# Four planning passes for the order of operations of a hybrid decoder step

## The chip, the cores and the metric

The kernel runs on one core of a Trainium2 chip. A core has five engines with an instruction list of their own: TensorE (PE; its weight loads PEld), VectorE (DVE), ScalarE (ACT), GpSimd (POOL) and SyncE (SP), which here issues the DMAs. Each works its list in order and waits for the others by semaphores. The metric is device time in microseconds of one execution, the median of several. Lower is better.

## The reference

Two groups of tokens (32 sample tokens and 512 of the prompt in each, T = 544 columns, the prompt's halves one after the other) pass two layers with D = 2048, all in fp32:

```python
def mixer_layer(x, ...):
    h = rmsnorm(x, norm_g)
    z = h @ w_in                       # 2048 x 5120
    u_a, v_a, g_a, q, k, v, g_b, u_c, g_c = jnp.split(z, splits, axis=-1)
    q, k = rope(q), rope(k)
    out_a = chunk_mlp(u_a, v_a, w_s, b_s)
    out_b = swa(q, k, v, sinks)        # window of 128, 16 heads, 4 kv heads
    out_c = s5(u_c, h0, ...)           # complex scan over the tokens, gelu, glu
    mixed = concat[out_a * silu(g_a), out_b * silu(g_b), out_c * silu(g_c)]
    return x + mixed @ w_out
```

A last RMSNorm gives y. New keys, values, chunk rows and scan states are outputs too.

## The kernel before

**Tiling.** Activations lie transposed: 16 tiles of 128 features by 544 tokens. An fp32 product is made of three fp32r products: each operand is split into a rounded part `hi` and a rest `lo` (ScalarE writes `hi`, VectorE subtracts), and hi·hi, hi·lo and lo·hi are added in PSUM. Weights are split when they arrive (tiles `wr` raw, `wh` and `ks` split); activations are split once per group (`gen_rows`, tiles `s`). For each layer and each of the two groups of tokens the code records:

- `input_tiles`: single output tiles, 16 contraction steps each (`project`), with the branches (attention, S5, chunk) recorded between them from generators in lanes. In the very first stage three tiles share the PSUM banks and are multiplied by the row `rstd` afterwards (`mul(t[:, sl], ps[h], rstd[:, sl])` and the rope of the keys); `rstd` itself is made from the same loaded rows (`gen_first`). `gen_tables(l)` builds the S5 tables of a layer with many small VectorE operations; layer 0's are recorded during the first stage, layer 1's during the second group's input stage of layer 0.
- `input_pairs` and then `output_tiles`: pairs of output tiles by seven half products (`product_pair`), 21 matmuls of 272 columns for each of 8 contraction steps, in seven PSUM banks. The first group of a layer also builds the weight sums on VectorE (`add(r[...])`, tile `wr`) and stores them; the second loads them back (`si`, `so`). At the end of a pair ScalarE copies the first product out (tile `e`), and VectorE's adds free the other banks one after the other. The next group's row splits are recorded from `after(k)`, which is called within a pair's steps, so ahead of that pair's adds.

**The order.** No instruction is issued while this is recorded. Line 202, `take`, stores each operation with its predecessors (by overlapping reads and writes, and by who had a buffer before) and a rank, `k - self.lead`, its place in the record less a lead. Weight loads and splits have a lead of 150 places, of 300 at the start of a stage (`rec.ahead(AHEAD)`, lines 860 and 907). Line 233, `times`, gives each a duration: `end`, until its result is there, and `step`, until its engine takes the next. Line 280, `order`, is a list scheduler: it steps through modelled time, and an engine that is free takes the lowest rank among the operations that are ready by then. An operation on another engine becomes ready `WAKE` after the end of what it waits for (32 to 65 ns). It has a model of the port that VectorE and GpSimd share, of a slower TensorE after a pause, of the DMA queue, and of ScalarE's table loads. Line 353, `give`, issues everything in that order; line 357 is the call, so all instructions of the profile carry L357 and are told apart by tile names. What is given to an engine stays in that order on the chip.

Of the kernel before, what the change touches and what calls it, by code (L numbers as in the profile page):

```python
# [75 lines left out]
ROW = {t: r for r, t in enumerate(ROWS)}  # L76
OUT_SINGLE = 2

SUMS_AT = 6
RES = 8  # L80
OUTRES = 4
# [54 lines left out]
class Recorder:  # L136
# [2 lines left out]

    ENGINES = ("SP", "Activation", "PE", "DVE", "Pool")  # L140

    WAKE = {"DVE": 32, "Activation": 32, "Pool": 65, "PE": 50, "SP": 50}
    TABLES = {AF.Exp: 0, AF.Tanh: 0, AF.Sin: 1, AF.Sqrt: 2, AF.Sigmoid: 3, AF.Silu: 4}

    class Engine:
# [133 lines left out]

    def order(self):  # L280

        n = len(self.ops)
        after = [[] for _ in range(n)]
        for k, preds in enumerate(self.preds):
            for j, written in preds.items():
                after[j].append((k, written))
        left, at = [len(p) for p in self.preds], [0.0] * n
        ready, come, free = ({e: [] for e in self.ENGINES}, {e: [] for e in self.ENGINES}, {e: 0.0 for e in self.ENGINES})
        for k in range(n):
            if not left[k]:  # L290
                heapq.heappush(ready[self.ops[k][0]], (self.ops[k][4], k))
        port = queue = idle = 0.0
        cold, table, events, out, flying = -1.0, None, [0.0], [], []
        while events:
            now = heapq.heappop(events)
            while events and events[0] <= now:
                heapq.heappop(events)
            for e in self.ENGINES:
                while come[e] and come[e][0][0] <= now + 1e-6:
                    k = heapq.heappop(come[e])[1]  # L300
                    heapq.heappush(ready[e], (self.ops[k][4], k))
            for e in self.ENGINES:
                if free[e] > now + 1e-6 or not ready[e]:
                    continue

                if e == "SP" and len(flying) >= 8 and flying[-8] > now:
                    heapq.heappush(events, flying[-8])
                    continue
                k = ready[e][0][1]
                end, step, lock, more = self.ops[k][5]  # L310
                if lock and e in ("DVE", "Pool") and port > now + 1e-6:
                    heapq.heappush(events, port)
                    others = [x for x in ready[e] if not self.ops[x[1]][5][2]]
                    if not others:
                        continue
                    ready[e].remove(min(others))
                    heapq.heapify(ready[e])
                    k = min(others)[1]
                    end, step, lock, more = self.ops[k][5]
                else:  # L320
                    heapq.heappop(ready[e])
                if lock:
                    port = now + step
                if e == "PE":

                    if now - idle > 1500 and now > 20000:
                        cold = now + (3400 if now - idle < 3500 else 6800)
                    if now < cold:
                        end, step = end * 1.6, step * 1.7
                    idle = now + step  # L330
                elif e == "SP":
                    queue = max(now + 600, queue) + more
                    end = queue + 1400 - now
                    flying.append(now + end)
                elif e == "Activation" and more is not None:
                    if more != table:
                        end, step = end + 1283, step + 1283
                    table = more
                out.append(k)
                free[e] = now + step  # L340
                heapq.heappush(events, free[e])
                for s, written in after[k]:
                    es = self.ops[s][0]
                    t = now + (step if es == e and (e == "PE" or e != "SP" and not written) else end + self.WAKE[es])
                    at[s] = max(at[s], t)
                    left[s] -= 1
                    if not left[s]:
                        heapq.heappush(come[es], (at[s], s))
                        heapq.heappush(events, at[s])
        assert len(out) == n  # L350
        return out

    def give(self, tc):
        with tc.manual_schedule():
# [6 lines left out]
def hybrid_step(ctx: ExitStack, tc: tile.TileContext, a, o):  # L361
# [14 lines left out]
    class Slots:  # L376
# [22 lines left out]
        def put(self, *xs):  # L399
            for x in xs:  # L400
                self.free.append(self.held.pop(id(x))[1])
# [387 lines left out]
    def gen_rows(source, scales, order, xs, acc, keep, norm):  # L789


        if norm is not None:
            rs = tt()
            SP.dma_start(rs, rs_d[norm])
        for n, k in enumerate(order):
            t = source(k)
            scale = None if scales is None else scales[:, k:k + 1]
            if norm is not None:
                V.scalar_tensor_tensor(out=t, in0=t, scalar=scale, in1=rs, op0=ALU.mult, op1=ALU.mult)
                SP.dma_start(xn_d[k], t)  # L800
                scale = None
                if n == KT - 1:
                    put(rs)
            if k < 8:
                xs[k] = [half(), half()]
                for h, sl in HS:
                    split(xs[k][h], t[:, sl], scale)
            else:
                xs[k] = row(t, scale)
            if acc is not None:  # L810
                sum_squares(t, acc, n == 0, t)
            if keep is None:
                put(t)
            else:
                keep[k] = t
            yield
# [83 lines left out]
    def project(tiles, xs, order=range(KT), ready=None, ps=None, first=0):  # L900

        ps = ps or [[mm_t.get() for h in range(2)] for _ in tiles]
        order = list(order)[:4 * len(tiles[0])]
        for c in range(len(tiles[0])):
            for n, chunks in enumerate(tiles):
                r, w = raw.part(), hl.part()
                with rec.ahead(FIRST_AHEAD if c < first else AHEAD):
                    SP.dma_start(r, chunks[c].rearrange("p (k m) -> p k m", k=4))
                    S.activation(w[:, 0], r, AF.Copy)
                    V.tensor_tensor(out=w[:, 1], in0=r, in1=f32(w[:, 0]), op=ALU.subtract)  # L910
                for j in range(4):
                    if ready is not None:
                        ready(order[4 * c + j])
                    x = xs[order[4 * c + j]]
                    for i, (p, q) in enumerate(((0, 0), (0, 1), (1, 0))):
                        for h in range(2):
                            TE.matmul(ps[n][h], w[:, p, j, :], x[h][q], start=c + j + i == 0, stop=4 * c + j == len(order) - 1 and i == 2)
                tick()
        return ps
# [418 lines left out]
    def input_tiles(l, g, X):  # L1338
# [9 lines left out]
        while n < len(order):  # L1348
# [81 lines left out]
            if two[-1] == (GLU_AFTER if l + g else ("va", 1)):  # L1430
# [17 lines left out]
                put(*ub)  # L1448
            if len(order) - n == SUMS_AT:
                lanes["ops"].add(X.sums(RES))  # L1450
# [276 lines left out]
```

## Time and profile before

| | |
|---|---|
| median of 3 runs | 3124.15 us (3121.15 to 3125.85) |
| profiled execution | 3125.5 us, span 3123.8 us |
| TensorE busy | 2962.7 us, 95%, 24208 matmuls |
| VectorE busy | 2400.8 us, 77% |
| ScalarE busy | 1567.3 us, 50% |
| GpSimd busy | 103.1 us, 3% |
| mean granted TensorE clock | 0.98 |
| HBM traffic | 610 MB, 195 GB/s over the span |

Busy time is the time in which an engine has at least one instruction at work. The clock is the share of TensorE's full clock that was granted: 1.00 is 2.4 GHz, 0.50 is 1.2 GHz, and a mean over a stretch lies between. The span runs from the first to the last instruction. Tile names are cut of their numbers: `s` are the general buffers, `e` those near the PSUM banks, `mm`, `sc` and `bk` PSUM banks, `wr`, `wh` and `ks` weights, `x`, `xn`, `br`, `mix` DRAM tensors.

### The profile page before, as it was taken

To read this page: it belongs to the slowest core of one execution; us is meant where nothing else is said; L and a number is where in the kernel's file an instruction comes from. 1 tells how busy PE (TensorE), PEld (TensorE's weight loads), DVE (VectorE), ACT (ScalarE), POOL (GpSimd) and SP (SyncE) were. 2 spreads that over 40 slices of the span, in tenths; PEclk is the share of its full clock that TensorE was granted. 3 is DMA by queue.
4 is the path that set the end of the run, shared out by engine and by line. 5 is a ranking of instruction groups with operands and counts; after the bars stand their busy time and mean duration, and the time that the engine had idled before them with its cause. 6 is when DMAs were issued, how large, how long until landed. Compare 5 with 4: busy or idle time off the path is not lost. (4 is left out here: it accounts for less than half of the span.)

```text
span 3123.8 us, 64427 instructions
## 1 busy us (share of the span) xinstructions
PE 2962.7 (95%) x24208; PEld 2880.1 (92%) x24208; DVE 2400.8 (77%) x4856; ACT 1567.3 (50%) x3106; POOL 103.1 (3%) x280
## 2 busy tenths in 40 slices
PE   5999999999898999999999999999999999999996
PEld 5988999989888899999999899999998999999996
DVE  9778789898997876668675877779887687556866
ACT  4347644453444764445443665335444475544643
POOL 0010000000010000000001000000000000000000
PEclk8999999999999999999999999999999999999998
DMA  5554376757964527667695335666679554667665
GB/s 176 182 165 124 100 247 232 241 188 238 309 196 131 153 85 231 197 227 227 219 315 148 108 111 173 223 227 227 212 255 315 162 150 137 199 199 232 214 216 174
DMA packets 394842, 614.29 MB, mean 197 GB/s; under 512 B 82209, under 2 KB 139169, under 8 KB 394529
## 3 DMA queue, kind: packets, MB, share of 16 engines
q1 hardware_dynamic: 394528, 610.17, 61.6%
q8 instruction: 189, 3.10, 0.4%
q14 instruction: 125, 1.02, 0.1%
HBM read 439.64 MB, written 170.38 MB: 195 GB/s over the span
## 5 line engine op out<-in xcount | busy, mean ns | idle before, releaser
L357 PE MATMUL mm<-s,wh 128*128 128x272 f32 x12660 | 1849.7, 293 | 67.6 <-ACT wh L357 23.2
L357 PEld LDWEIGHTS mm<-s,wh 128*128 128x128 f32 x12660 | 1695.8, 191 | 90.3 <-ACT wh L357 29.8
L357 ACT ACTIVATE wh<-wr 128x896 fp32r<-128x896 f32 (+1 forms) x719 | 567.5, 795 | 762.0 <-PE mm L357 511.2
L357 DVE TENSOR_TENSOR wh<-wr,wh 128x896 fp32r<-128x896 f32 (+1 forms) x719 | 640.2, 895 | 321.8 <-ACT wh L357 306.5
L357 PE MATMUL sc<-s,wh 128*128 128x272 f32 x2346 | 513.0, 290 | 0.8 <-DVE e L357 0.7
L357 DVE TENSOR_TENSOR s<-s,s 128x544 f32<-128x544 f32 (+11 forms) x738 | 387.7, 552 | 35.5 <-DMA yd<-s 9.9
L357 PE MATMUL mm<-s,ks 128*128 128x272 f32 x2316 | 388.2, 289 | 6.1 <-ACT ks L357 3.0
L357 PEld LDWEIGHTS sc<-s,wh 128*128 128x128 f32 x2346 | 384.3, 190 | 2.9 <-DVE e L357 2.7
L357 PEld LDWEIGHTS mm<-s,ks 128*128 128x128 f32 x2316 | 327.3, 189 | 9.1 <-DVE e L357 3.7
L357 ACT ACTIVATE ks<-wr 128x896 fp32r<-128x896 f32 x193 | 183.2, 949 | 235.4 <-PE mm L357 131.7
L357 DVE TENSOR_TENSOR ks<-wr,ks 128x896 fp32r<-128x896 f32 x193 | 209.9, 1088 | 108.5 <-ACT ks L357 97.5
L357 PE MATMUL sc<-s,ks 128*128 128x272 f32 x1158 | 258.5, 290 | 1.1 <-DVE e L357 0.9
L357 PE MATMUL bk<-s,wh 128*128 128x272 f32 x1125 | 256.7, 291 | 2.7 <-DVE e L357 2.6
L357 DVE TENSOR_TENSOR wr<-wr 128x256 f32<-128x256 f32 (+1 forms) x432 | 219.2, 508 | 39.6 <-DMA wr<-w_inp 21.2
L357 ACT ACTIVATE s<-s 128x544 fp32r<-128x544 f32 (+4 forms) x320 | 171.2, 555 | 102.1 <-DVE s L357 60.8
L357 ACT ACTIVATE s<-s,mx 128x128 f32<-128x128 f32 x512 | 177.5, 389 | 34.2 <-DVE mx L357 33.8
L357 PEld LDWEIGHTS sc<-s,ks 128*128 128x128 f32 x1158 | 191.0, 189 | 3.3 <-DVE e L357 3.0
L357 PEld LDWEIGHTS bk<-s,wh 128*128 128x128 f32 x1125 | 185.7, 190 | 4.3 <-DVE e L357 4.0
L357 PE MATMUL bk<-s,s 128*64 128x128 f32 (+6 forms) x2048 | 173.8, 272 | 4.7 <-DVE s L357 4.1
L357 ACT ACTIVATE s<-e 128x544 fp32r<-128x544 f32 (+1 forms) x192 | 122.9, 653 | 99.7 <-DVE e L357 95.1
L357 PEld LDWEIGHTS bk<-s,s 128*64 128x64 f32 (+3 forms) x2048 | 149.3, 151 | 18.3 <-DVE s L357 4.9
L357 PE MATMUL bk<-cst,s 128*128 128x128 f32 (+1 forms) x448 | 99.0, 304 | 45.3 <-ACT s L357 19.4
(129 smaller groups left out, 2286.4 us busy)
## 6 DMA issues: line engine op xcount, KB each, us to landing
wr<-w_ins SPq DMA_DIRECT2D x296, 256.0 KB, 3.0
s<-x SPq DMA_DIRECT2D x184, 272.0 KB, 4.2
wr<-w_inp SPq DMA_DIRECT2D x176, 256.0 KB, 3.0
si<-wr SPq DMA_DIRECT2D x176, 256.0 KB, 3.0
wr<-si SPq DMA_DIRECT2D x168, 256.0 KB, 2.9
wr<-w_inp SPq DMA_DIRECT2D x168, 192.0 KB, 3.3
wr<-w_outp SPq DMA_DIRECT2D x112, 256.0 KB, 3.0
so<-wr SPq DMA_DIRECT2D x112, 256.0 KB, 2.9
```

Source lines behind the costliest of these rows:

```text
L357: call(*[self.real(*x) if x[1] else x[0] for x in args], **{n: self.real(*x) if x[1] else x[0] for n, x in kw.items()})
```

## The change

`order` becomes a loop of four passes. `forward(rank)` is the old scheduler with its ranks given from outside; it also returns each operation's modelled start and the modelled end of all. `backward(starts)` runs the list from its end: an operation is ready when all that follow it are placed, an engine takes the one that started last in the forward pass, and the result is, for each operation, a latest start, counted back from the end. These are the ranks of the next forward pass. The first pass has the recorded ranks with their lead; the later ones have no lead. The start times of the pass with the earliest modelled end give the order that is issued. Beside it the `WAKE` times grow by 100 ns, by 200 for TensorE and the DMA queue. No operation, shape, buffer or DMA is added or taken away.

```diff
--- before.py
+++ after.py
@@ -76,6 +76,8 @@
 ROW = {t: r for r, t in enumerate(ROWS)}
 OUT_SINGLE = 2
 
+PASSES = 4
+
 SUMS_AT = 6
 RES = 8
 OUTRES = 4
@@ -139,7 +141,7 @@
 
     ENGINES = ("SP", "Activation", "PE", "DVE", "Pool")
 
-    WAKE = {"DVE": 32, "Activation": 32, "Pool": 65, "PE": 50, "SP": 50}
+    WAKE = {"DVE": 132, "Activation": 132, "Pool": 165, "PE": 250, "SP": 250}
     TABLES = {AF.Exp: 0, AF.Tanh: 0, AF.Sin: 1, AF.Sqrt: 2, AF.Sigmoid: 3, AF.Silu: 4}
 
     class Engine:
@@ -279,7 +281,67 @@
 
     def order(self):
 
+        best, rank = None, [x[4] for x in self.ops]
+        for _ in range(PASSES):
+            end, starts = self.forward(rank)
+            if best is None or end < best[0]:
+                best = end, starts
+            rank = self.backward(starts)
+        return sorted(range(len(self.ops)), key=lambda k: (best[1][k], k))
+
+    def backward(self, starts):
+
         n = len(self.ops)
+        left, at, when = [0] * n, [0.0] * n, [0.0] * n
+        for preds in self.preds:
+            for j in preds:
+                left[j] += 1
+        ready, come, free = ({e: [] for e in self.ENGINES}, {e: [] for e in self.ENGINES}, {e: 0.0 for e in self.ENGINES})
+        for k in range(n):
+            if not left[k]:
+                heapq.heappush(ready[self.ops[k][0]], (-starts[k], k))
+        events, port, queue = [0.0], 0.0, 0.0
+        while events:
+            now = heapq.heappop(events)
+            while events and events[0] <= now:
+                heapq.heappop(events)
+            for e in self.ENGINES:
+                while come[e] and come[e][0][0] <= now + 1e-6:
+                    k = heapq.heappop(come[e])[1]
+                    heapq.heappush(ready[e], (-starts[k], k))
+            for e in self.ENGINES:
+                if free[e] > now + 1e-6 or not ready[e]:
+                    continue
+                k = heapq.heappop(ready[e])[1]
+                end, step, _, more = self.ops[k][5]
+
+                if e == "SP":
+                    queue = max(now + 1400, queue) + more
+                    end = queue + 600 - now
+                when[k] = now + step
+                free[e] = now + step
+                heapq.heappush(events, free[e])
+                for j, written in self.preds[k].items():
+                    ej = self.ops[j][0]
+                    d = self.ops[j][5]
+
+                    if ej == e and (e == "PE" or e != "SP" and not written):
+                        t = now + step
+                    elif ej == "SP":
+                        t = now + step + self.WAKE[e] + 1400 + 600 - 385
+                    else:
+                        t = now + step + self.WAKE[e] + d[0] - d[1]
+                    at[j] = max(at[j], t)
+                    left[j] -= 1
+                    if not left[j]:
+                        heapq.heappush(come[ej], (at[j], j))
+                        heapq.heappush(events, at[j])
+        return [-x for x in when]
+
+    def forward(self, rank):
+
+        n = len(self.ops)
+        starts, last = [0.0] * n, 0.0
         after = [[] for _ in range(n)]
         for k, preds in enumerate(self.preds):
             for j, written in preds.items():
@@ -288,7 +350,7 @@
         ready, come, free = ({e: [] for e in self.ENGINES}, {e: [] for e in self.ENGINES}, {e: 0.0 for e in self.ENGINES})
         for k in range(n):
             if not left[k]:
-                heapq.heappush(ready[self.ops[k][0]], (self.ops[k][4], k))
+                heapq.heappush(ready[self.ops[k][0]], (rank[k], k))
         port = queue = idle = 0.0
         cold, table, events, out, flying = -1.0, None, [0.0], [], []
         while events:
@@ -298,7 +360,7 @@
             for e in self.ENGINES:
                 while come[e] and come[e][0][0] <= now + 1e-6:
                     k = heapq.heappop(come[e])[1]
-                    heapq.heappush(ready[e], (self.ops[k][4], k))
+                    heapq.heappush(ready[e], (rank[k], k))
             for e in self.ENGINES:
                 if free[e] > now + 1e-6 or not ready[e]:
                     continue
@@ -337,6 +399,8 @@
                         end, step = end + 1283, step + 1283
                     table = more
                 out.append(k)
+                starts[k] = now
+                last = max(last, now + end)
                 free[e] = now + step
                 heapq.heappush(events, free[e])
                 for s, written in after[k]:
@@ -348,7 +412,7 @@
                         heapq.heappush(come[es], (at[s], s))
                         heapq.heappush(events, at[s])
         assert len(out) == n
-        return out
+        return last, starts
 
     def give(self, tc):
         with tc.manual_schedule():
```

## Rows read from the trace of the kernel before

**Rows 1.** The page, its first lines: span, busy time of each engine.

```profile
span 3123.8 us, 64427 instructions
...
PE 2962.7 (95%) x24208; PEld 2880.1 (92%) x24208; DVE 2400.8 (77%) x4856; ACT 1567.3 (50%) x3106; POOL 103.1 (3%) x280
```

**Rows 2.** Stretches by stage: busy us (instructions) per engine, clock, DMA.

```profile
core 0: us, PE busy (x) PEld busy (x) DVE busy (x) ACT busy (x) POOL busy (x), PEclk, DMA share, GB/s
390.50:859.10 468.60, 436.74 (x3345) 426.95 (x3342) 414.17 (x772) 213.71 (x318) 2.56 (x2) 0.97 0.73 243
1952.50:2421.10 468.60, 446.85 (x3437) 437.59 (x3438) 387.47 (x680) 209.98 (x307) 4.62 (x10) 0.98 0.74 243
...
1249.60:1562.00 312.40, 312.28 (x2484) 311.66 (x2483) 216.57 (x330) 149.33 (x198) 0.00 (x0) 1.00 0.68 218
2733.50:3045.90 312.40, 312.05 (x2479) 311.02 (x2478) 212.63 (x320) 153.30 (x206) 0.00 (x0) 1.00 0.68 215
...
842.00:1178.00 336.00, 316.30 (x2765) 299.88 (x2765) 273.71 (x746) 188.80 (x503) 23.42 (x62) 0.97 0.51 152
2372.00:2673.00 301.00, 297.71 (x2604) 285.00 (x2603) 215.93 (x502) 168.59 (x444) 13.45 (x37) 1.00 0.58 173
```

**Rows 3.** Stretches, columns as in rows 2: head, three ends of groups.

```profile
56.00:74.60 18.60, 1.12 (x5) 0.71 (x4) 18.50 (x90) 1.06 (x3) 0.00 (x0) 0.50 0.27 86
826.00:842.00 16.00, 9.56 (x53) 8.59 (x51) 16.00 (x36) 7.59 (x18) 2.12 (x1) 0.79 0.93 323
1596.00:1612.00 16.00, 10.44 (x64) 10.00 (x63) 16.00 (x34) 7.33 (x17) 1.70 (x1) 0.79 0.99 353
2355.00:2372.00 17.00, 9.87 (x53) 9.26 (x52) 17.00 (x33) 9.59 (x22) 1.77 (x2) 0.72 1.01 370
```

**Rows 4.** Instructions in order of time, the head: start, us, engine, operation.

```profile
55.81 0.67 ACT L357 COPY rstd<-bk 128x512 f32<-128x512 f32 x2 [3.24 <-PE bk L357]
...
58.99 0.74 DVE L357 TENSOR_TENSOR s<-s,s 128x64 f32<-128x64 f32 x6
...
68.40 5.89 DVE L357 TENSOR_TENSOR s<-s,s 128x256 f32<-128x256 f32 x9
...
74.20 0.44 DVE L357 TENSOR_TENSOR s<-mm,rstd 128x272 f32<-128x272 f32 x1
...
74.69 5.50 PE L357 MATMUL mm<-s,wh 128*128 128x272 f32 x27 [1.22 <-DVE s L357]
```

**Rows 5.** Instructions in order of time, end of a group; [idle before, who ended it].

```profile
2356.62 0.39 ACT L357 COPY e<-mm 128x272 f32<-128x272 f32 x1 [0.70 <-PE mm L357]
...
2358.15 2.12 DVE L357 TENSOR_TENSOR s<-s,s 128x272 fp32r<-128x272 f32 x5
...
2362.26 0.61 ACT L357 ACTIVATE wh<-wr 128x512 fp32r<-128x512 f32 x1
...
2364.32 0.68 DVE L357 TENSOR_TENSOR wh<-wr,wh 128x512 fp32r<-128x512 f32 x1
...
2364.96 0.82 PE L357 MATMUL mm<-s,wh 128*128 128x272 f32 x2 [6.63 <-ACT wh L357]
...
2368.19 0.43 DVE L357 TENSOR_TENSOR e<-mm,e 128x272 f32<-128x272 f32 x1
```

**Rows 6.** Slices of the span, columns as in rows 2.

```profile
78.10:156.20 78.10, 75.13 (x670) 73.09 (x670) 54.75 (x107) 28.04 (x60) 6.92 (x15) 0.97 0.60 182
2186.80:2264.90 78.10, 72.44 (x543) 71.23 (x542) 68.08 (x119) 34.69 (x46) 0.00 (x0) 0.96 0.66 212
```

**Rows 7.** The chain that ended last, its end: start, us, what.

```profile
3107.62 8.48 DVE s L357 x8
```

**Rows 8.** Who waited for whom: us in total, times, longest.

```profile
DVE wr L357 <- DMA wr<-w_inp: 21.2, 21, 2.8
```

**Rows 9.** Groups of ScalarE instructions: busy us, mean ns, idle before.

```profile
L357 ACT ACT_TABLE_LOAD x29 | 37.2, 1283 | 4.9 <-DVE mx L357 3.7 <-PEq L1723 0.8
```

**Rows 10.** Instructions in order of time, first group's pairs.

```profile
587.50 0.69 DVE L357 TENSOR_TENSOR wr<-wr 128x512 f32<-128x512 f32 x1 [2.77 <-DMA wr<-w_inp]
588.11 1.08 DVE L357 TENSOR_TENSOR wh<-wr,wh 128x896 fp32r<-128x896 f32 x1
...
589.11 0.42 DVE L357 TENSOR_TENSOR wr<-wr 128x256 f32<-128x256 f32 x1
589.45 0.43 DVE L357 TENSOR_TENSOR e<-mm,e 128x272 f32<-128x272 f32 x1
...
589.94 0.52 PE L357 MATMUL mm<-s,wh 128*128 128x272 f32 x2 [4.03 <-DVE e L357]
```

## The prediction

> **What bounds the kernel now.** I read the page's busy line first: TensorE is busy 95% of the span, VectorE 77%, ScalarE half [rows 1]. So time can come only from TensorE's last 5% and from its clock. The work on it is fixed: the change alters no instruction's shape and no count, only the order in which each engine gets its list.
>
> Then the table of stretches. Where TensorE runs dense, 2484 matmuls take 312.4 us, 0.126 us each, with no idle time and the clock at its upper level [rows 2]. There VectorE is busy 69%. In the crowded stretches, the first group's pairs of each layer, VectorE is busy 83 to 88% and TensorE stands idle for 31.9 and 21.8 us, at a mean clock of 0.97 and 0.98 [rows 2]. The same first-group/second-group contrast shows that the loss is not TensorE's own: it waits for VectorE.
>
> Then what VectorE does while TensorE waits. Two pictures repeat.
>
> The head: rstd, the row of reciprocal norms, lands at 56.5 us. The multiply by it that frees the first PSUM bank starts at 74.2 us. Between the two VectorE is busy for 18.5 of 18.6 us with 90 instructions of S5 table building (s<-s,s of 64 to 256 columns), and TensorE does 1.12 us of work at a clock of 0.50, the 1.2 GHz level [rows 3, 4]. The tables come first only because they were recorded earlier: the rank is the place in the record.
>
> The ends of a group: ScalarE has copied the first product out at 2356.6 us. VectorE's next step, the add that frees the second bank, starts at 2368.2 us, behind row splits of the next group, which were recorded earlier. ScalarE's next weight piece waits until 2362.3 us, VectorE's half of it ends at 2365.0 us, and TensorE stands 6.63 us [rows 5]. In three such stretches VectorE is 100% busy and TensorE does 53, 64 and 53 matmuls in 16, 16 and 17 us [rows 3].
>
> **The change part by part.** All terms are against the profiled execution, 3125.5 us around a span of 3123.8 us; the median shown, 3124.15 us, is 1.35 us lower, so I take that off at the end.
>
> *Ranks from the backward pass.* An operation's rank becomes its latest start, so whatever TensorE waits for next outranks work that is due later. This removes no instruction, and I cost it stretch by stretch.
>
> Head. The tables are needed only by S5, whose first projection is the fifth of the list. If the two multiplies by rstd run at 56.5 us, matmuls resume at about 57.5 instead of 74.7 us [rows 4]: 17 us at most. I take 15, since part of the resumed work still runs at the lower clock. The 18 us of table work move to the next slice, where VectorE is busy 54.75 of 78.10 us, so 23 us are free [rows 6]; if that cover fails, S5's transposes are late and the gain can shrink to nothing. Bounds 0 and -17. **-15.**
>
> Ends of groups. At 0.126 us, 53, 64 and 53 matmuls are 6.7, 8.1 and 6.7 us, so 9.3, 7.9 and 10.3 us are lost, 27.6 in all, half-speed clock included [rows 3]. The evacuation and the next weights can go ahead of all but the first row splits, but the rows are wanted there too and VectorE is full; so I take half. Bounds 0 and -27. **-14.**
>
> Layer 1's tables. They are recorded in the second group's input stage of layer 0. From the end of the first burst to the same small matmul of the chunk branch this stage takes 336 us, and a layer later, without tables, 301 us: VectorE is busy 273.7 against 215.9 us, TensorE idle 19.7 against 3.3 us, at clocks of 0.97 and 1.00 [rows 2]. Idle time (16.4) and clock (0.03 x 336 = 10.1) make 26.5 us; the rest of the 35 is work that stays. The tables' deadline is a stage later, behind dense stretches where VectorE has 96 us free (312.4 - 216.6), but their buffers are handed on in recorded order, which holds some of them back. Bounds 0 and -26; I take half. **-13.**
>
> Pairs of the first groups. Idle time without the two ends of groups is 25.4 + 14.6 us; the clock's share (0.03 and 0.02 of 468.6 us, less the same two ends) is 10.7 + 4.6; together 55 us [rows 2, 3]. VectorE must still build the weight sums there, with two raw buffers, and part of the stalls are late transfers that no rank mends. I take a quarter. Bounds 0 and -55. **-14.**
>
> Tail. After the last matmul the chain is norm, multiplies, output: VectorE's multiplies alone are 8.48 us of it [rows 7]. Everything there already waits for the thing before it. **0**, bounds -3 and +3.
>
> *Waits given time to spare.* A handover costs 100 ns more in the planner's account (200 for TensorE and the queue); on the chip nothing is added. It moves an instruction that would be only just ready behind one that is. No row shows such a wait alone; the nearest are the waits of VectorE for late w_inp transfers, 21.2 us in 21 waits, the longest 2.8 us [rows 8]. Bounds -21 and +21; 100 ns cover few of these, so **0**.
>
> *The lead of weight loads.* AHEAD (150 places) and FIRST_AHEAD (300) enter only the first pass. With ranks of latest starts the weights keep whatever urgency their matmuls have. The buffers (two raw, three split) allow at most a few steps ahead in either order, so **0**; from the other side, the price if they come late is the slower rival's.
>
> *ScalarE's table loads* may grow from 29; each is 1283 ns [rows 9] on an engine that is half idle: 0, and 29 more would be 37 us of ScalarE's 1550 us free.
>
> Row and rule at one place: at 587.5 us VectorE has stood 2.77 us for a transfer of w_inp, with the bank-freeing add two instructions further on its list, and TensorE stands 4.03 us for that add [rows 10]. The Trainium skill (TensorE: Matmul & The Clock Gate, section on the array's architecture, engine queue depths) says that ScalarE and VectorE are strict first-in, first-out. The trace agrees: the add did not pass the waiting one. By that rule a better plan cannot mend a misjudged transfer, and a plan with less slack is hit harder.
>
> Sum: -15 - 14 - 13 - 14 = -56; 3125.5 - 56 = 3069.5, less 1.35 for the median: **3068 us**.
>
> **The rivals.**
>
> *Slower: weights just in time.* If the ranks let other work in front of weight splits in the dense stretches (1249.6 to 1562 and 2733.5 to 3045.9 us), they come to look like the slice from 2186.8 us: 5.66 us idle and 0.04 of 78.1 us of clock, 8.8 us [rows 6]. Eight such slices are 70 us; less the 56 gained it is +14: 3138 us. It decides from 7 us per dense slice on. For it: TensorE's idle time there is below 0.4 us per 312, so there is only something to lose. Against it: VectorE has 31% free there and the pass is greedy, so what is ready is not held back. Chance 0.12.
>
> *Nothing moves.* The emitted order is the pass with the earliest modelled end, and the first pass still has the old ranks. If the later ones come out longer, the program keeps its record's order with longer waits, VectorE's 18.5 us of tables stay in the head, and the time is 3124 us, give or take 10. For it: recorded order has served 95%. Against it: the two pictures above are plain faults of rank. Chance 0.12.
>
> *Much faster.* If nearly all of what VectorE's order costs goes: -17 - 27 - 26 - 55 = -125; short of that by a sixth for late transfers, 3020 us. Against it: VectorE stays at 83 to 88% in the pairs. Chance 0.12.
>
> **How the numbers follow.** The forecast has 0.64. Its own range: with -17, -20, -22 and -30 it is 3035; with -10, -7, 0 and -5 it is 3102. The range of 8 in 10 runs from 3020 (half of the much faster case lies below) to 3127, above which lie the slower case and a little of the unmoved one. About 0.2%, 6 us, is what can be told from no change. Faster: 0.64 + 0.12 + a third of the unmoved case = 0.80; same 0.08; slower 0.12.
>
> **What would show it.** Right: the multiply by rstd within 3 us of its landing, with table building behind it; the three ends of groups with over 90 matmuls in the same length; layer 0's second input stage at under 10 us of idle time; dense stretches still at 0.126 us. Wrong: the head's gap still there (no new ranks), idle time and clock of over 7 us in a dense slice (weights late), or VectorE's gaps moved to another place with the sum of TensorE's idle time unchanged at 161 us (3123.8 - 2962.7 [rows 1]).

## The result, and the profile after

| | before | after |
|---|---|---|
| device time, median of 4 runs | 3123.65 us (3121.15 to 3125.85) | 3036.74 us (3033.21 to 3039.77) |
| ratio to before, 95% interval | | 0.9722 (0.9705 to 0.9738) |
| profiled run; its span | 3125.5; 3123.8 us | 3033.21; 3031.5 us |
| mean granted clock of TensorE | 0.980 | 0.988 |

The change gains 87 us; the forecast was 56, a time of 3068 us. The 3036.74 us lie inside the range, and the sign and the likeliest case held; the size was a third too small. The measured time is nearer to the much faster rival's 3020 us than to the forecast.

The page of the changed kernel, its first lines:

```profile
span 3031.5 us, 64421 instructions
...
PE 2935.6 (97%) x24208; PEld 2865.8 (95%) x24208; DVE 2392.2 (79%) x4856; ACT 1559.9 (51%) x3106; POOL 120.1 (4%) x280
```

Against [rows 1]: the same 24208 matmuls. TensorE's idle time (span less busy) goes from 161.1 to 95.9 us, and its busy time from 2962.7 to 2935.6 us. The first is waiting that went. The second, 27.1 us, fits the clock: the same matmuls run at a mean of 0.988 instead of 0.980, and 0.020 of 3123.8 less 0.012 of 3031.5 us is 26 us. 65.2 + 27.1 = 92.3 us, the difference of the two spans. The other engines do what they did.

Stretches of the changed kernel by stage, columns as in [rows 2]. First the head and the three ends of groups, then layer 0's and layer 1's second input stage, then the two dense stretches:

```profile
56.00:72.00 16.00, 15.60 (x113) 15.54 (x113) 15.90 (x69) 5.37 (x10) 0.00 (x0) 0.89 0.27 68
...
787.00:803.00 16.00, 14.52 (x96) 14.52 (x97) 15.97 (x46) 12.31 (x28) 0.36 (x1) 0.79 0.95 336
1549.00:1565.00 16.00, 13.80 (x96) 13.37 (x95) 8.29 (x17) 6.94 (x14) 0.00 (x0) 0.89 0.97 321
2274.00:2291.00 17.00, 13.88 (x97) 13.46 (x96) 17.00 (x33) 9.50 (x21) 2.71 (x1) 0.90 0.90 310
...
809.00:1121.00 312.00, 302.81 (x2693) 287.36 (x2691) 268.26 (x717) 182.06 (x494) 27.19 (x62) 0.99 0.52 158
2295.00:2584.00 289.00, 288.87 (x2554) 278.67 (x2553) 215.22 (x498) 166.35 (x441) 14.26 (x38) 1.00 0.58 179
...
1195.00:1505.00 310.00, 310.00 (x2477) 310.00 (x2476) 215.61 (x330) 148.81 (x198) 0.00 (x0) 1.00 0.69 221
2655.40:2965.00 309.60, 309.35 (x2469) 308.99 (x2468) 214.26 (x328) 153.71 (x208) 0.00 (x0) 1.00 0.67 215
```

In the head TensorE now runs 113 matmuls in 16 us, where [rows 3] have 5 in 18.6 us. The three ends have 96, 96 and 97 in the lengths that had 53, 64 and 53, although VectorE is still 100% busy in two of them. How these stretches are laid matters: from 783 us the first has 74, from 2268 us the third has 82. A count that does not depend on it is that of the last 60 us before each norm sum at a group's end: 337, 403 and 381 matmuls before the change, 391, 446 and 405 after it. That is 121 more, which is 15 us at 0.126 us each. Layer 0's second input stage takes 312 us instead of 336, with 9.2 us idle instead of 19.7 [rows 2]. The dense stretches still run at 0.125 us a matmul.

The head of the changed kernel in order of time (start, us, engine, operation):

```profile
51.38 4.61 DVE L421 TENSOR_TENSOR s<-s,s 128x512 f32<-128x512 f32 x5
51.45 0.59 ACT L421 COPY rstd<-bk 128x512 f32<-128x512 f32 x1 [1.13 <-PE bk L421]
...
52.73 0.19 ACT L421 COPY rstd<-bk 128x32 f32<-128x32 f32 x1 [0.69 <-PE bk L421]
...
55.91 0.43 DVE L421 TENSOR_TENSOR s<-mm,rstd 128x272 f32<-128x272 f32 x1
...
56.40 1.25 PE L421 MATMUL mm<-s,wh 128*128 128x272 f32 x5 [0.74 <-DVE s L421]
```

The second copy of rstd ends at 52.92 us; the multiply starts 3.0 us later, behind five table products, the first of which VectorE had begun, instead of 17.7 us later [rows 4]. The end of a group that [rows 5] show, after the change:

```profile
2278.36 0.94 PE L421 MATMUL mm<-s,ks 128*128 128x272 f32 x4 [3.08 <-ACT ks L421]
...
2282.63 1.42 DVE L421 TENSOR_TENSOR s<-s,s 128x272 fp32r<-128x272 f32 x3
...
2283.20 0.39 ACT L421 COPY e<-mm 128x272 f32<-128x272 f32 x1
...
2285.27 0.43 DVE L421 TENSOR_TENSOR e<-mm,e 128x272 f32<-128x272 f32 x1
```

The add that frees the bank comes 2.1 us after ScalarE's copy, not 11.6; a stall of 3.08 us for a weight piece is what is left of 6.63.

Where the 92 us of span came from, by the same instruction in both traces (us from the start of the span). The small matmul of the chunk branch is the one that reads tile `wss`; the norm sums are the matmuls that sum the squares for the RMSNorm at a group's end:

| marker on TensorE | before | after | gained up to here |
|---|---|---|---|
| first small matmul of the chunk branch, layer 0, group 0 | 91 | 72 | 19 |
| norm sums after (layer 0, group 0) | 863 | 830 | 33 |
| the small matmul, (layer 0, group 1) | 1178 | 1121 | 57 |
| norm sums after (layer 0, group 1) | 1631 | 1573 | 57 |
| the small matmul, (layer 1, group 0) | 1911 | 1841 | 70 |
| norm sums after (layer 1, group 0) | 2393 | 2316 | 77 |
| the small matmul, (layer 1, group 1) | 2673 | 2584 | 89 |
| end of the span | 3123.8 | 3031.5 | 92 |

The borders are soft, since TensorE's own list is reordered too. But the pattern is plain: every stage of a first group and every input stage gives something; the stretch with the dense part gives nothing in layer 0 and 3 us in layer 1.

### The profile page after: what moved, and what is told of

Same layout as the page of the kernel before. It is cut to its first block, busy times and chain, and to the rows that moved or that the text cites. A ratio compares the mean times of both kernels' runs of the same rounds, so it can differ in the third digit from the quotient of the medians.

```text
span 3031.5 us, 64421 instructions
## 1 busy us (share of the span) xinstructions
PE 2935.6 (97%) x24208; PEld 2865.8 (95%) x24208; DVE 2392.2 (79%) x4856; ACT 1559.9 (51%) x3106; POOL 120.1 (4%) x280
## 4 chain that ended last, share of the span: by engine, by line
PE 59%; DVE 6%; DMA 2%; ACT 1%; issue 1%; DVEq 0%; SPq 0%; ACTq 0%
PE mm L421 38%; PE sc L421 11%; PE bk L421 10%; DVE s L421 3%; DVE e L421 1%; ACT s L421 1%; DVE wh L421 1%; DVE wr L421 1%; DMA wr<-w_outp 1%; DMA wr<-w_inp 0%; DMA si<-wr 0%; ACT wh L421 0%; DVE ks L421 0%; DMA br<-s 0%; DMA s<-mix 0%
## 5 line engine op out<-in xcount | busy, mean ns | idle before, releaser
L421 DVE TENSOR_TENSOR s<-s,s 128x272 fp32r<-128x272 f32 (+11 forms) x738 | 391.5, 556 | 30.7 <-ACT s L421 10.5
L421 PE MATMUL mm<-s,ks 128*128 128x272 f32 x2316 | 396.8, 290 | 13.4 <-ACT ks L421 12.2
L421 PE MATMUL bk<-s,s 128*64 128x128 f32 (+6 forms) x2048 | 182.0, 272 | 5.3 <-ACT s L421 2.7
L421 DVE TENSOR_TENSOR s<-e,s 128x544 fp32r<-128x544 f32 (+1 forms) x176 | 132.4, 769 | 3.8 <-ACT s L421 2.9
```

Of the source, the lines that this page charges most:

```text
L421: call(*[self.real(*x) if x[1] else x[0] for x in args], **{n: self.real(*x) if x[1] else x[0] for n, x in kw.items()})
```

## The experiments

Theory: the ranks gain by undoing the stalls that the prediction names, and the waits do nothing. Rivals: the waits carry part of it; the gain is one move (tables, ends) and not the joint order; it is VectorE's order alone. In the edits shown, lines that do not matter are left out (`...`). Each ratio is against runs of the kernel before on the same chip.

**The two halves apart.** One alone on the old program, the other alone on the new:

```
e1, on the kernel before:
-    WAKE = {"DVE": 32, "Activation": 32, "Pool": 65, "PE": 50, "SP": 50}
+    WAKE = {"DVE": 132, "Activation": 132, "Pool": 165, "PE": 250, "SP": 250}
e2, on the changed kernel: the same line, the other way round
```

> Old scheduler in one pass with recorded ranks, WAKE times raised as in the change (132, 132, 165, 250, 250 ns). Theory A (ranks pay, waits add nothing, the prediction's term of 0): within 8 us of before, 3116 to 3132 us, and the head's 18 us gap still there. Rival B (the 31 us that the result is better than the forecast come from the waits): 3085 to 3100 us, with TensorE's idle time outside the head down by 20 us or more.

> Four passes with the old WAKE times (32, 32, 65, 50, 50 ns). Theory A (ranks pay): within 10 us of the changed kernel, 3030 to 3047 us. Rival B (waits pay a third): 3060 to 3075 us, most of the loss as short stalls of TensorE behind VectorE and ScalarE in the pairs of the first groups.

Waits alone: 3099.12 us, ratio 0.9934 (0.9918 to 0.9951), -22 us. Passes alone: 3055.18 us, 0.9788 (0.977 to 0.9806), -66 us, between the two ranges named for it. Together -87: the two add up. So the waits are not worth nothing. TensorE's idle time falls by 15.2 us with the waits alone (161.1 to 145.9). Two kinds of waits that shrink there (waiter, what it waits for; us in total, times, longest), the first of them in the kernel before and in the waits-only kernel, the second in the waits-only kernel:

```profile
PEld bk L357 <- ACT s L357: 36.0, 85, 2.0
```

```profile
PEld bk L357 <- ACT s L357: 15.2, 39, 2.3
...
DVE wr L357 <- DMA wr<-w_inp: 8.9, 10, 2.1
```

The second was 21.2 us in 21 waits [rows 8]; the same wait for w_outp grew meanwhile, from 9.4 to 13.1 us. The first, TensorE's weight loads waiting for a tile that ScalarE is just finishing, was open to be read, and the prediction did not use it. It does not explain what the waits give on top of the new ranks. There it is short already, and what shrinks is waits for VectorE (passes-only kernel, then the changed one):

```profile
PEld bk L421 <- DVE s L421: 27.3, 29, 4.6
...
PEld bk L421 <- ACT s L421: 10.4, 33, 1.4
```

```profile
PEld bk L421 <- DVE s L421: 18.7, 17, 3.8
...
PEld bk L421 <- ACT s L421: 12.2, 26, 2.9
```

**Which wait.** On the changed kernel, only some of the longer waits:

```
e7   WAKE = {"DVE": 32, "Activation": 32, "Pool": 65, "PE": 250, "SP": 50}
e8   WAKE = {"DVE": 132, "Activation": 132, "Pool": 165, "PE": 50, "SP": 250}
e10  the old WAKE, and 100 ns more on the edges from a DMA's landing alone, in both directions:
-    t = now + step + self.WAKE[e] + 1400 + 600 - 385
+    t = now + step + self.WAKE[e] + 100 + 1400 + 600 - 385
...
-    ... else end + self.WAKE[es])
+    ... else end + self.WAKE[es] + (100 if e == "SP" else 0))
```

> The changed kernel with the long wait for TensorE alone (250 ns; the others 32, 32, 65, 50). Theory C (the spare time pays where TensorE, the bound, would be given an instruction that is not quite ready and stands behind it): 3036 to 3044 us, as the changed kernel. Rival D (it pays in keeping VectorE, ScalarE and the queue from standing behind a late arrival): 3050 to 3060 us, as with no longer wait at all.

> The changed kernel with the long waits for all but TensorE (132, 132, 165, SP 250; TensorE 50 ns). Theory C: 3050 to 3060 us. Rival D: 3034 to 3044 us. If both this and the run with TensorE's wait alone lie between 3040 and 3050 us, the gain is shared.

> Four passes, old WAKE times, and 100 ns more only where an engine waits for a DMA's landing. Theory F (the longer waits pay as cover for late landings): 3036 to 3044 us. Rival G (they pay in the handovers between ScalarE, VectorE, GpSimd and the queue): 3050 to 3060 us, as without them.

TensorE's longer wait alone: 3058.89 us, 0.9803 (0.9784 to 0.9822), the time of the passes alone. All but TensorE's: 3037.45 us, 0.9731 (0.9717 to 0.9746), the whole gain. Landings alone: 3048.09 us, 0.9776 (0.976 to 0.9793); the interval overlaps that of the passes alone, so at most a part. VectorE's waits for late weights, in the passes-only kernel, then with landings alone, then with all but TensorE's wait:

```profile
DVE wr L421 <- DMA wr<-w_inp: 18.1, 17, 2.4
DVE wr L421 <- DMA wr<-w_outp: 16.1, 14, 2.9
```

```profile
DVE wr L421 <- DMA wr<-w_outp: 9.2, 14, 1.3
...
DVE wr L421 <- DMA wr<-w_inp: 8.0, 9, 2.3
```

```profile
DVE wr L421 <- DMA wr<-w_outp: 12.6, 13, 2.6
...
DVE wr L421 <- DMA wr<-w_inp: 9.4, 14, 1.5
```

100 ns on the landings cut these waits from 34.2 to 17.2 us, as far as the fuller set does (22.0 us), yet the fuller set is 11 us faster. So late transfers are not the whole of it; spare time on the handovers between the engines, or the queue's own 200 ns, must carry the rest. Which of these was not separated.

**Single moves on the kernel before.** Each takes one stall that the prediction names and mends it by hand, by moving that work back or ahead in the record. The last one moves the end of every pair ahead, not only the ends of groups:

```
+    def later(gen, n):
+        while True:
+            with rec.ahead(-n):
+                if next(gen, gen) is gen:
+                    return
+            yield
e3: -    lanes["misc"].add(gen_tables(0))
    +    lanes["misc"].add(later(gen_tables(0), 150))
e5: -                lanes["misc"].add(gen_tables(l + 1))
    +                lanes["misc"].add(later(gen_tables(l + 1), 500))
e6: the eight operations at the end of product_pair that empty the banks:
+        with rec.ahead(150):
             S.copy(t[:, 0, :], p1)
             add(c1[:, 0:HALF], p2, t[:, 0, :])
...
```

> Kernel before, but layer 0's table operations are ranked 150 places later, nothing else. Theory (the head is a plain fault of rank): 3102 to 3110 us, a gain of 15 to 20; the first multiply by rstd starts within 3 us of the landing of rstd, and the gain is kept to the end. Rival (VectorE is the bound of the head and its next slice, so the table work comes back as a wait of S5): 3118 to 3127 us, with the gap moved to between 80 and 160 us.

> Kernel before, but layer 1's table operations are ranked 500 places later, nothing else. The prediction's term (their place in the record costs 13 us): 3104 to 3114 us, with TensorE's idle time in the second input stage of layer 0 down from 19.7 to under 10 us. Rival (as for layer 0's tables: an operation moved alone meets a deadline of its buffers or of S5, and the loss moves): 3118 us or more, S5's matmuls late in the same stage.

> Kernel before, but the eight operations that empty the PSUM banks at the end of a pair are ranked 150 places earlier, nothing else. The prediction's term (the adds behind the next group's row splits cost 14 us at the ends of groups): 3100 to 3112 us, over 80 matmuls in each of the three stretches. Rival (VectorE is full there, rows and weights are wanted as much, so the add's place is not what TensorE waits for): 3116 to 3127 us.

Layer 0's tables later: 3128.17 us, 1.0032 (1.002 to 1.0045). The head's gap is gone, the multiply by rstd starts at 53.35 us, but the sigmoids of the GLU come at 293 us instead of 284, and the whole is 7 us slower. The prediction had named a condition: "if that cover fails, S5's transposes are late". Up to 100 us TensorE has done 608 matmuls here, 460 in the kernel before; up to 160 us it is 1026 and 1025, up to 200 us 1284 and 1366. So what the head gains is lost between 100 and 200 us. A stretch of the kernel before, the same of this kernel's profiled run (it took 3141.14 us, its longest run, so the sizes may not be typical), columns as in [rows 2], and TensorE in order of time at its start:

```profile
130.00:160.00 30.00, 30.00 (x286) 29.22 (x286) 21.68 (x42) 8.86 (x21) 2.74 (x8) 1.00 0.63 192
```

```profile
130.00:160.00 30.00, 30.00 (x190) 25.08 (x191) 10.61 (x26) 4.76 (x15) 2.31 (x8) 0.72 0.44 133
```

```profile
129.09 0.39 PE L357 MATMUL mm<-s,wh 128*128 128x272 f32 x1
129.41 0.57 PE L357 MATMUL bk<-s,s 128*32 128x112 f32 x2
129.91 0.39 PE L357 MATMUL mm<-s,wh 128*128 128x272 f32 x1
130.23 0.24 PE L357 MATMUL bk<-s,s 128*32 128x16 f32 x2
```

VectorE is busy 10.61 of 30 us, so its cover did not fail. The narrow matmuls (128 x 32 weights) build the tables' kernels. With their rank moved back they take turns with the ordinary ones on a TensorE that is never idle: 190 matmuls where the kernel before does 286 in the same 30 us. Over the whole profiled run TensorE's idle time is shorter than before, 148.8 against 161.1 us, and its busy time 27.9 us longer. At the upper level of the clock the next matmul starts 0.32 us behind an ordinary one that a narrow one follows (129.09 to 129.41), against 0.125 in a dense stretch. In the kernel before each 32 of them run as one block of 1.58 us, and in the changed kernel they do so again, as this row shows:

```profile
112.05 1.58 PE L421 MATMUL bk<-s,s 128*32 128x16 f32 x32
```

So this run does not price the head by itself: the move by hand also breaks TensorE's blocks. It does not show that the head is worth nothing; with VectorE's ranks alone (below) the head is mended without that.

Layer 1's tables later: 3147.77 us, 1.0088 (1.0072 to 1.0104), 28 us slower. Two of TensorE's waits in this kernel, in the state products of layer 0's own S5:

```profile
904.56 1.18 PE L357 MATMUL sc<-s,s 128*64 128x68 f32 x16 [4.73 <-DMA s<-ud]
...
934.24 2.08 PE L357 MATMUL sc<-s,s 128*64 128x68 f32 x32 [6.59 <-DVE s L357]
```

These are 11.3 us in a stage whose small matmul comes at 1201 us, 23 later than before. Why a later table block makes that work late isn't settled; VectorE is busy less there, 67.0 of the 80 us from 860 us on, against 76.0. But such waits are the smaller part. From 940 to 1080 us TensorE is as busy as in the kernel before and does 159 matmuls fewer, 20 us at 0.126 (kernel before, then this one):

```profile
940.00:1080.00 140.00, 128.05 (x1147) 118.25 (x1147) 114.32 (x266) 84.38 (x243) 11.18 (x31) 0.95 0.46 130
```

```profile
940.00:1080.00 140.00, 128.77 (x988) 117.77 (x987) 111.33 (x247) 73.76 (x206) 16.36 (x35) 0.89 0.39 115
```

From 1029 us on it alternates narrow and ordinary matmuls there too, as with layer 0's tables. Over the whole profiled run its idle time is the old one (162.5 against 161.1 us); the longer span is busy time. So this move, too, breaks TensorE's blocks, and what follows is only that the -13 of this term cannot be had by pushing the tables back as a block, at the one distance tried.

Bank-emptying first: 3120.48 us over 10 runs, 1.0002 (0.9989 to 1.0014). The stretches of [rows 3] in this kernel:

```profile
826.00:842.00 16.00, 14.85 (x101) 14.40 (x101) 16.00 (x31) 7.67 (x18) 0.43 (x1) 0.87 0.93 334
1596.00:1612.00 16.00, 15.39 (x120) 15.05 (x120) 14.94 (x29) 8.52 (x18) 0.00 (x0) 1.00 0.93 333
2355.00:2372.00 17.00, 15.48 (x118) 15.04 (x117) 15.05 (x30) 9.21 (x19) 0.70 (x2) 0.98 0.91 304
```

101, 120 and 118 matmuls: in these stretches the stalls that I priced at 27.6 us are mended as well as by the change, over the 80 matmuls that the theory asked for, and the time does not move. The interval excludes a gain of more than 4 us. Part of the reason is that a stall went next door. In the 20 us just ahead of the third stretch, the kernel before and then this one:

```profile
2335.00:2355.00 20.00, 19.25 (x151) 18.81 (x150) 19.71 (x36) 11.07 (x19) 0.00 (x0) 1.00 0.95 321
```

```profile
2335.00:2355.00 20.00, 13.59 (x97) 13.11 (x96) 19.23 (x33) 12.23 (x25) 0.00 (x0) 0.94 1.02 370
```

Over the last 60 us before each norm sum this kernel does 356, 463 and 380 matmuls, 1199 against 1121 before and 1242 with the change: 10 us of the change's 15, and none at the third end. The medians show nothing of these 10 us, and why isn't settled: the profiled run is the fastest of this kernel's ten, and the edit also moves the ends of all other pairs.

**Whose order.** From the pass that would be emitted, the late-start ranks are given to some engines alone, the recorded ranks to the others, and one more forward pass is made (old waits):

```
-                best = end, starts
+                best = end, starts, rank
...
+        rank = [best[2][k] if x[0] == "DVE" else x[4] for k, x in enumerate(self.ops)]
+        best = self.forward(rank)
e11: if x[0] in ("DVE", "Activation")
```

> Old WAKE times; four passes are made, then one more forward pass in which VectorE alone has the late-start ranks of the best pass and all other engines have the recorded ranks. Theory A (what paid is VectorE's order, as the prediction says): 3055 to 3070 us, at least 50 of the 66 us that the four passes gave with these waits. Rival E (the orders pay only together: VectorE's new order meets ScalarE, the queue and TensorE in the old one): over 3085 us. Between: shared.

> As the run with late-start ranks on VectorE alone (3085 us), but VectorE and ScalarE have them; TensorE, GpSimd and the queue keep recorded ranks; old WAKE times. Theory H (the rest of the ranks' gain lies between the two engines that make TensorE's operands, the softmax on ScalarE first): 3055 to 3065 us, TensorE's waits for ScalarE's softmax rows under 5 us. Rival I (it lies in TensorE's own order or the queue's): 3077 us or more.

VectorE alone: 3085.37 us, 0.9895 (0.988 to 0.991), -34 us. VectorE and ScalarE: 3086.82 us, 0.9895 (0.9876 to 0.9913), the same. Passes for all engines had -66. With VectorE's ranks the head is mended (multiply at 54 us, the first small matmul at 70), but TensorE's transposes still wait (those of the attention's softmax rows above all, which ScalarE makes; the chunk branch and the tables have some too). In the kernel before, the VectorE-only kernel and the passes-only kernel (busy us, mean ns, idle before, by releaser):

```profile
L357 PE MATMUL bk<-cst,s 128*128 128x128 f32 (+1 forms) x448 | 99.0, 304 | 45.3 <-ACT s L357 19.4 <-issue 16.3 <-DVE s L357 9.3
```

```profile
L423 PE MATMUL bk<-cst,s 128*128 128x128 f32 (+1 forms) x448 | 95.7, 296 | 18.8 <-ACT s L423 11.4 <-DVE s L423 7.2
```

```profile
L421 PE MATMUL bk<-cst,s 128*128 128x128 f32 (+1 forms) x448 | 86.1, 285 | 8.9 <-DVE s L421 6.0 <-ACT s L421 2.5
```

Of the 45.3 us before, 16.3 are a single wait in the head; the other 29 fall to 18.8 and 8.9. So half of what the ranks give comes with VectorE's ranks alone; the other half needs the ranks of TensorE, the queue or GpSimd, alone or together with ScalarE's, which these runs don't tell apart.

**More passes, better prices.**

```
e4    PASSES = 2
e12   PASSES = 8, and in the planner's prices:
+     t += 82 if len(ins) > len(wide) else 0      (ScalarE, an operand per partition)
+     t += 62 if method == "scalar_tensor_tensor" and len(ins) > len(wide) else 0      (VectorE)
      1400 -> 1900 for a landing, in all three places
```

> The changed kernel with two passes instead of four: ranks of latest starts taken once. Theory A (the first set of late-start ranks mends the order, the rest is polish): 3036 to 3050 us. Rival (each pass moves a part, as the work slides stage by stage): 3060 to 3085 us.

> The changed kernel with costs read from its trace: ScalarE's operations with a scale or bias per partition 82 ns longer, VectorE's scalar_tensor_tensor with such an operand 62 ns, a landing 500 ns later, and eight passes. Theory G (the longer waits cover what the planner's costs leave out, so better costs give more): 3022 to 3032 us. Rival J (what is left is VectorE's and the buffers' bound): 3033 to 3043 us, as the changed kernel.

Two passes: 3046.80 us, 0.9764 (0.9747 to 0.978), 74 of the 87 us; passes 3 and 4 give the other 13. Eight passes with prices nearer to the trace: 3031.87 us, 0.9722 (0.9704 to 0.974). The time lies in the range that its theory names, but the kernel before ran at 3116.73 us beside it, so the ratio is that of the change, and nothing was gained. No version had a better ratio than the change.

## Why the prediction was right in kind and too small

**What bounds it: held.** TensorE's idle time and clock were the only room, and all of the gain is there (65.2 + 27.1 us).

**Waits, 0: the step that failed.** The bounds were -21 and +21; the runs gave -22 alone and about -20 on top of the ranks. Of the 31 us that the forecast lacks, this term is 21. I took [rows 8], VectorE's waits for late weights, as the nearest row and argued that 100 ns cover few of them. Two things were wrong. The plan does not cover a wait, it chooses another order in which the waiter is not next; waits far longer than 100 ns went (21.2 to 8.9 us on that row). And one row was too narrow: in the old order TensorE's 85 waits for ScalarE, 36.0 us, fell to 15.2. In the new order that row stays short with and without the longer waits, and the shorter waits are those for VectorE and for transfers, so which row should have priced the term there is open. TensorE's own longer wait gave nothing.

**Ranks, -56: -66 measured.** As sizes of stretches three of the four terms are near the mark and the pairs are not; as separate causes the terms were not borne out. The sizes below are read from the changed kernel, so they contain the waits' share.

- Head, -15: the gap from rstd's landing to the multiply shrank by 14.7 us. rstd itself lands 3.6 us earlier, which I did not price; together the 19 us at the first marker.
- Ends, -14: at 0.126 us a matmul the stretches now lose 3.9, 3.9 and 4.8 us, 12.6 in place of 27.6: -15, and the 60 us before each norm sum give the same 15. But moved ahead by hand the ends gain nothing in all (the runs above), so the figure is what the stretch shows, not what the move earns.
- Layer 1's tables, -13: by the prediction's own measure, idle time and clock above those of the same stage a layer later, the loss falls from 26.5 to 12.2 us: -14. The stage is 24 us shorter, but with 72 matmuls fewer, which now run outside it. That the tables are simply too early is not shown as a cause that stands alone: moved back as a block they cost 28 us.
- Pairs, -14: by the prediction's measure (idle time and clock of the first groups' stretches without the two ends, of the same length and as far from the norm sums) 55 us become about 36 (31.7 idle, 4.3 clock): -19, the term that was sized too small.
- No term: what all these leave of the 92 us is some 25. Part of it lies in the input stages of layer 1, which are 12 and 13 us shorter and which I had not priced, since TensorE stood idle for only 3.3 us in the one that I looked at. That stage now has 50 matmuls fewer, so part of its gain is work that TensorE does elsewhere. Mean idle and clock per stage showed me only where TensorE stood, not that its own list could hold other work ready.
- Tail, 0: from the last norm sums to the end it is 25.6 us in both traces. Lead of weight loads, 0: the dense stretches are unharmed. ScalarE's table loads: 29 as before.

**The rivals.** Weights just in time (slower) fell: the dense stretches have 0.0 and 0.3 us idle. A trace of it is there, TensorE's waits for ScalarE's ks pieces grew from 3.0 to 12.2 us, but in the crowded stretches. Nothing moves fell with the head. Much faster (3020) came nearer than the forecast: I had 125 us less a sixth, and the stated obstacle, VectorE's load in the pairs, did leave stalls.

**The signs named ahead** all came: 3.0 us from landing to multiply, 96, 96 and 97 matmuls, 9.2 us idle, 0.125 us a matmul, idle time not unchanged. The first held only just, and not with all the table building behind it; the matmuls at the ends depend on how the stretch is laid (74 to 97).

## What to carry to other kernels

When a planner gets a better rank, price its joint effect: stalls that one sees in the trace mark where a list is wrong, but moving one block past them by hand can earn nothing (ends) or lose (tables). Look then at TensorE's matmuls per stretch and not at its idle time alone: in both runs with later tables the loss is busy time. Spare time in the planner's handovers is worth a term of its own; look for it in all rows of short, frequent waits, TensorE's for ScalarE and VectorE too, and not in those for transfers alone. Two passes already bring most of it.

## What the runs showed of the hardware

TensorE can be slow without being idle. In the kernel with layer 0's tables later, a row of the same trace (columns as in [rows 2]):

```profile
116.00:126.70 10.70, 10.70 (x87) 10.70 (x87) 10.30 (x33) 3.48 (x6) 2.38 (x7) 1.00 0.74 206
132.00:148.00 16.00, 16.00 (x65) 12.13 (x65) 1.96 (x3) 1.72 (x9) 0.20 (x1) 0.50 0.37 115
```

From 132 to 148 us it is busy all the time, and yet at 0.50, the 1.2 GHz level, with 65 matmuls. Before that it was at 1.00, and from 127.6 to 138.4 us it alternated single ordinary matmuls with pairs of narrow ones; its weight loads are busy 5.70 us of these 10.80. The switch itself costs time, 0.32 us against 0.125 at the upper level. The fall is not a single case. In the same kernel such an alternation begins at 92.5 us, and the clock is 1.00 from 88.4 to 92.4 us and 0.50 from 97.5 to 99.9 us. In the kernel with layer 1's tables later one begins at 1029.0 us:

```profile
1022.00:1029.00 7.00, 7.00 (x58) 6.85 (x56) 6.63 (x15) 4.16 (x8) 0.00 (x0) 1.00 0.31 77
1033.50:1036.00 2.50, 2.50 (x10) 1.41 (x9) 0.00 (x0) 0.63 (x1) 0.00 (x0) 0.50 0.00 0
```

So at three places in two profiled runs the lower level follows the alternation with no idle time of TensorE between. That the alternation brought the clock down fits this, and is not shown, since no run changes it alone.

An operand per partition costs ScalarE time that the planner had not counted. In the changed kernel, without and with one (busy us, mean ns):

```profile
L421 ACT ACTIVATE s<-s 128x544 fp32r<-128x544 f32 x72 | 46.2, 650 | 25.5 <-DVE s L421 14.3 <-DMA s<-mix 7.5 <-issue 1.7
...
L421 ACT ACTIVATE s<-s,ng 128x544 fp32r<-128x544 f32 x8 | 5.9, 734 | 0.0
```

84 ns each. Corrected in the plan, along with a later landing and more passes, it bought no measurable time.
